# A hybrid decoder step: the first inverse level of the recurrence on VectorE, another order of its value products, longer column fills, query columns behind the last preparation

## The chip, the core and the metric

The kernel runs on one core of one Trainium2 chip. The metric is the device time of one execution in microseconds (us). Before the change the median of three runs is 954.7 us (953.11, 954.70 and 957.25).

## What is computed

One layer of a decoder reads 1,024 prompt positions of width 1,024 and eight single-token samples. After an RMS norm, one projection w_in yields the columns of three head groups: sparse attention (NSA) with 8 query heads, a memory attention, and RWKV-7, a recurrence with 4 heads of 64. Their gated outputs go through w_out. The change touches the recurrence:

```python
def step(s, inp):
    r_t, k_t, v_t, w_t, kk_t, b_t = inp
    sa = jnp.einsum('bhvk,bhk->bhv', s, -kk_t)
    s = s * w_t[:, :, None, :] + sa[..., None] * b_t[:, :, None, :] + v_t[..., None] * k_t[:, :, None, :]
    return s, jnp.einsum('bhvk,bhk->bhv', s, r_t)
s_fin, ys = lax.scan(step, s0, xs)
```

The kernel works in chunks of 64 positions instead of single ones. Inside a chunk the coupling of the positions is a triangular 64 by 64 matrix per head, and the chunk needs its inverse.

## The kernel before

**Phase 1** (about the first 480 us) projects the columns, in tiles of 128 columns, and runs the recurrence between them. The 1,024 positions are four quarters, Q = 0 to 3. For each quarter `rwkv_prep` forms decays, keys and the products AM of one chunk position with another (p_am in PSUM, masked into AM by VectorE at L824), and `rwkv_state` inverts, solves and moves the state on. A quarter has four chunks: two pairs t, and in each pair two chunks p, on the upper or the lower 64 partitions. With four heads h that makes 16 triangular matrices at a time.

**The inverse** has levels. The 64 by 64 matrix is cut into two diagonal blocks of 32 by 32, and within these, levels i = 0 to 4 join blocks of 1, 2, 4, 8 and 16. All 32 blocks of 32 by 32 lie side by side as one tile of 128 partitions by 8 by 32. Level i is: product p_iy = AM times T (32 small matmuls of 32 by 32), mask on VectorE into iY (L857), a fill, product p_it of iY with the transposed T (32 matmuls again), copy by ScalarE into T (L895) and transposition by VectorE into Tt (L896), a fill. Level 0 is shorter: T is the identity there, its product copies AM into PSUM, the mask follows, and the result only has to be transposed (L878). Then come the joining of the two 32-blocks (p_iy and p_it with 16 matmuls each), p_x (inverse times right-hand sides), p_g, and four rounds of p_z (the state) with p_yy (outputs). Between the steps, work that does not wait for the inverse is placed: p_bt (turned keys), and p_r, the products with the values V (L872; 8 matmuls of 64 by 64 for a pair t).

**Order of the work.** TensorE's instructions run in the order in which `InOrder` receives them. `drive` (L598) takes a piece of the recurrence; the piece yields a number n, and `drive` then draws n times SLACK (1.3) us of column projections from the generator `columns` before the next piece. A step of `columns` counts as 0.7. These projections (p_pr, three matmuls for each 128 rows of input) are called fills. ORDER lists the column tiles in the order in which they are drawn: 0 to 5 keys and values, 6 to 9 queries (four tiles), 10 and 11 memory queries, 12 gates, 13 to 20 output gates z. The first EARLY = 17 are drawn beside the recurrence, the other four later.

A projected query tile is worked on for each half H of the positions: ScalarE copies it out, TensorE turns it (p_tk), ScalarE squares it (L375), then VectorE runs `norm_rope`: a reduction (L377), an inverse square root of 12 small instructions (L126 to L137), two multiplications (L383, L384) and six for the rotation (L396 to L399). SyncE stores it (L439). A z tile costs VectorE one or two instructions (L319) per half. Each tile of weights is split into two parts by ScalarE (whi, L283) and VectorE (wlo, L284).

For the other engines a scheduler sets the order; within an engine everything runs in that order, so one instruction that waits holds up all that stand behind it. The scheduler ranks what the recurrence issues ahead of the columns' work. PSUM tiles of the recurrence rotate through three buffers (pool pw).

After Q = 3, `rwkv_close` stores the state (S_out, on SyncE's queue), the pools of the recurrence end, and key blocks are read back (kd, SyncE) for the attention of phase 2; phase 3 is the output projection.

Of the kernel before, what the change touches and what calls it, by code (L numbers as in the profile page):

```python
# [10 lines left out]
F32 = mybir.dt.float32  # L11
# [9 lines left out]
T = 1024  # L21
# [7 lines left out]
ORDER = [4, 1, 11, 2, 3, 6, 5, 7, 13, 17, 10, 9, 15, 8, 0, 14, 12, 18, 16, 19, 20]  # L29
# [19 lines left out]
def bc(ap, shape):  # L49
    return ap.to_broadcast(shape)  # L50
# [64 lines left out]
class Step:  # L115
# [566 lines left out]
    def rwkv_open(self):  # L682
# [8 lines left out]
        self.eye = cm[:, 448:480]  # L691
        self.wa2 = c.tile([128, 256], F32, name="wa2")
# [135 lines left out]
    def rwkv_state(self, Q):  # L828
# [6 lines left out]
        blocks = [(2 * p + b, slice(p * 64 + b * 32, p * 64 + b * 32 + 32), p, b) for p in range(2) for b in range(2)]  # L835
        for g, o, p, b in blocks:
            x = AM[o, 2 * p:2 * p + 2, :, b * 32:b * 32 + 32]
            V.tensor_tensor(x, x, bc(self.eye[o, None, None, :], [32, 2, 4, 32]), op=OP.add)
        th = [(t, h, t * 4 + h) for t in range(2) for h in range(4)]
        bkT, pre = [None] * 2, {}  # L840
        for t in range(2):
            pt = self.pw.tile([128, 4, 64], F32, name="p_at", tag="w")
            for c in range(2):
                PE.transpose(pt[:, 2 * c:2 * c + 2, :].rearrange("p a b -> p (a b)"),
                             ar[:, c, t, 0].rearrange("p s e -> p (s e)"), I[:])
            pre[t] = self.rs.tile([128, 4, 128], F32, name="R", tag=f"R{t}")
            A.activation(pre[t][:, :, 0:64], pt[:], AF.Copy)
        yield 1.0
        T = Tt = None
        for i in range(5):  # L850
# [6 lines left out]
            V.tensor_tensor(Y[:], ps[:], bc(self.levels[:, i:i + 1, :], [128, 8, 32]), op=OP.mult)  # L857
            if i < 2:
                t = i
                pb = self.pw.tile([128, 2, 2, 128], F32, name="p_bt", tag="w")  # L860
                for c in range(2):
                    for p in range(2):
                        PE.transpose(pb[:, c, p, :], bk[:, c, 2 * t + p].rearrange("p a b -> p (a b)"), I[:])
                bkT[t] = self.rs.tile([128, 2, 2, 128], F32, name="bkT", tag=f"bkT{t}")
                A.activation(bkT[t][:], pb[:], AF.Copy)
            elif i < 4:
                t = i - 2
                pr = self.pw.tile([128, 4, 64], F32, name="p_r", tag="w")
                for p in range(2):
                    o, k = slice(p * 64, p * 64 + 64), slice(64 - p * 64, 128 - p * 64)  # L870
                    for h in range(4):
                        PE.matmul(pr[o, h, :], AM[k, 2 * p + t, h, 0:64], UV[k, 2 * t + p, h, :], start=True, stop=True)  # L872
                A.activation(pre[t][:, :, 64:128], pr[:], AF.Copy)
            yield 0.7
            new = [self.ri.tile([128, 8, 32], F32, name="iT", tag=f"iT{j}", bufs=2) for j in range(2)]
            flat = lambda x: x[:].rearrange("p j e -> p (j e)")
# [21 lines left out]
            yield 0.7  # L898
# [10 lines left out]
        yield 0.8  # L909
# [6 lines left out]
        yield 0.8  # L916
# [14 lines left out]
        for t in range(2):  # L931
# [18 lines left out]
            yield 0.7  # L950
# [1447 lines left out]
def host_consts():  # L2398
# [74 lines left out]
```

## Time and profile before

| | us |
|---|---|
| median of three runs | 954.7 |
| the profiled execution, its own time | 954.09 |
| its span, first to last instruction | 952.2 |
| TensorE (PE) busy in it | 914.3 |
| VectorE (DVE) busy | 647.6 |
| ScalarE (ACT) busy | 435.9 |
| the four calls of `rwkv_state`, about | 98 to 142, 183 to 227, 288 to 333, 372 to 419 |

The granted clock of TensorE is 0.996 of full speed over the span. Times in the trace are counted from the span's start. In the timeline a row joins several instructions; its second number is the time from the start of the first to the end of the last, and neighbouring rows of PE overlap at their ends, so the cost of a group is read from its start to the start of the next group. The trace counts two records for each matmul on plain f32 operands: 32 matmuls are x64. In square brackets stands idle time ahead of a row and what ended it.

### The profile page before, as it was taken

How to read it: one execution, taken by the hardware profiler on the slowest of the kernel's cores; microseconds unless marked ns; L12 is line 12 of the kernel's file. 1: busy time of each engine (PE TensorE's matmuls, PEld its weight loads, DVE VectorE, ACT ScalarE, POOL GpSimd, SP SyncE). 2: the span in 40 equal slices, each digit the busy share in tenths (PEclk: the TensorE clock that was granted, in tenths of full speed). 3: DMA queues.
4: the chain of work that ended last, by engine and by line, in shares of the span. 5: the costliest groups of instructions: out<-in, count | busy, mean ns of one | idle time of the engine just before them, and what ended most of it. 6: DMA issues, size and time to landing. Idle time of an engine off the chain costs nothing.

```text
span 952.2 us, 24814 instructions
## 1 busy us (share of the span) xinstructions
PE 914.3 (96%) x9911; PEld 779.8 (82%) x9911; DVE 647.6 (68%) x2017; ACT 435.9 (46%) x979; POOL 178.7 (19%) x270
## 2 busy tenths in 40 slices
PE   8999999999999998999998899999999999999998
PEld 7998888868888787787876788788888887887976
DVE  7668579837593699673447866757677996548564
ACT  7564324232442243222434676576666775424311
POOL 2000000000000000000001453454345665212111
PEclk9999999999999999999999999999999999999999
DMA  8421305221421116137436623251210035976661
GB/s 277 132 68 37 100 13 143 59 54 45 115 79 59 35 56 166 54 84 194 111 90 177 193 69 124 72 170 30 70 41 7 11 112 133 349 240 210 189 238 47
DMA packets 134987, 105.94 MB, mean 111 GB/s; under 512 B 34673, under 2 KB 121272, under 8 KB 134744
## 3 DMA queue, kind: packets, MB, share of 16 engines
q1 hardware_dynamic: 129880, 92.64, 33.2%
q0 software_dynamic: 3200, 10.49, 3.1%
q8 instruction: 78, 1.28, 0.5%
q10 hardware_dynamic: 1792, 1.23, 0.4%
q14 instruction: 37, 0.30, 0.1%
HBM read 85.74 MB, written 22.78 MB: 114 GB/s over the span
## 4 chain that ended last, share of the span: by engine, by line
PE 72%; DVE 16%; ACT 6%; DMA 3%; issue 2%; POOL 1%; SPq 0%; DVEq 0%; ACTq 0%; POOLq 0%
PE p_pr L87 20%; PE p_out L87 9%; PE p_pr L307 7%; PE p_s L87 5%; PE p_pT L87 4%; PE p_o L87 4%; PE p_hid L87 3%; ACT p L1399 2%; DVE p L1398 2%; PE p_z L87 2%; PE p_iy L87 2%; PE p_sc L87 1%; PE p_it L87 1%; PE p_tk L87 1%; PE p_q L87 1%
## 5 line engine op out<-in xcount | busy, mean ns | idle before, releaser
L87 PE MATMUL p_pr<-h,whi 128*128 128x512 f32 (+2 forms) x976 | 238.1, 337 | 0.0
L87 PEld LDWEIGHTS p_pr<-h,whi 128*128 128x128 f32 x976 | 158.1, 189 | 16.2 <-issue 2.2
L87 PE MATMUL p_pr<-h,wlo 128*128 128x512 f32 (+2 forms) x488 | 157.5, 326 | 0.6 <-DVE wlo L284 0.6
L1424 POOL TENSOR_SCALAR p<-p,fac,gates 128x640 f32<-128x640 f32 (+7 forms) x128 | 103.7, 821 | 106.8 <-DVE fac L1421 59.9
L1399 ACT ACTIVATE p<-p,nm 128x640 f32<-128x640 f32 (+7 forms) x128 | 93.0, 728 | 53.6 <-DVE nm L1398 46.1
L87 PEld LDWEIGHTS p_pr<-h,wlo 128*128 128x128 f32 x488 | 91.6, 189 | 9.1 <-DVE wlo L284 0.8
L87 PE MATMUL p_pT<-ident,p 128*128 128x128 f32 x528 | 71.9, 281 | 5.0 <-ACT pt L1369 1.6
L1073 POOL MEMSET w2d<- 128x128 f32 x1 | 0.2, 206 | 397.0 <-DVE rq_t L136 397.0
L1398 DVE CUSTOM_DVE_ANT_0 p<-p_s,bmask 128x512 f32<-128x512 f32 (+7 forms) x96 | 60.3, 661 | 18.5 <-PE p_s L87 16.6
L87 PEld LDWEIGHTS p_pT<-ident,p 128*128 128x128 f32 x528 | 57.7, 142 | 16.0 <-issue 6.4
L307 PE MATMUL p_pr<-h,whi 128*128 128x264 f32 (+2 forms) x320 | 68.3, 309 | 0.4 <-ACT whi L283 0.4
L87 PE MATMUL p_o<-pt,vs 128*64 128x128 f32 x1056 | 67.9, 277 | 0.4 <-DVE cat L1457 0.4
L87 PE MATMUL p_s<-kh,qs 128*128 128x512 f32 (+3 forms) x191 | 65.5, 355 | 1.0 <-DVE nm L1398 1.0
L284 DVE TENSOR_TENSOR wlo<-wraw,whi 128x1024 fp32r<-128x1024 f32 x33 | 40.4, 1223 | 33.3 <-ACT whi L283 33.2
L87 PEld LDWEIGHTS p_o<-pt,vs 128*64 128x64 f32 x1056 | 57.0, 137 | 7.2 <-issue 3.8
L87 PE MATMUL p_s<-kl,qs 128*128 128x512 f32 (+3 forms) x192 | 60.4, 335 | 0.0
L283 ACT ACTIVATE whi<-wraw 128x1024 fp32r<-128x1024 f32 x34 | 36.0, 1058 | 53.4 <-PE p_pr L87 43.8
L1371 DVE COPY pt<-p_pT 128x512 f32<-128x512 f32 (+1 forms) x72 | 48.3, 674 | 13.8 <-PE p_pT L87 13.1
L307 PEld LDWEIGHTS p_pr<-h,whi 128*128 128x128 f32 x320 | 51.1, 189 | 3.2 <-ACT whi L283 0.8
L87 PE MATMUL p_out<-woh,chi 128*128 128x512 f32 x128 | 51.7, 404 | 0.0
L87 PE MATMUL p_out<-woh,clo 128*128 128x512 f32 x128 | 50.2, 392 | 0.4 <-DVE clo L2311 0.4
L87 PE MATMUL p_out<-wol,chi 128*128 128x512 f32 x128 | 49.9, 390 | 0.0
(553 smaller groups left out, 1921.8 us busy)
## 6 DMA issues: line engine op xcount, KB each, us to landing
wraw<-in_w_in_dram SPq DMA_DIRECT2D x34, 512.0 KB
pg<-in_c_pool_dram SPq DMA_DIRECT2D x32, 256.0 KB
pg<-in_c_pool_dram SPq DMA_DIRECT2D x48, 128.0 KB
x<-in_x_prompt_dram SPq DMA_DIRECT2D x8, 512.0 KB
z_d<-zt SPq DMA_DIRECT2D x16, 256.0 KB
cat<-z_d SPq DMA_DIRECT2D x8, 512.0 KB
xres<-in_x_prompt_dram POOLq DMA_DIRECT2D x16, 256.0 KB, 3.7
out_dram<-xres POOLq DMA_DIRECT2D x16, 256.0 KB, 3.0
```

Source lines behind the costliest of these rows:

```text
L87: self.last = getattr(self.engine, op)(*a, **k)
L283: nc.scalar.activation(hi[:, :, :n], raw[:, :, :n], AF.Copy)
L284: (low or nc.vector).tensor_tensor(lo[:, :, :n], raw[:, :, :n], hi[:, :, :n].bitcast(F32), op=OP.subtract)
L307: self.last_mm = self.pe.matmul(ps[:m, :b - a], w[:, k, :m], h[k][:, a:b], start=(k == 0 and i == 0), stop=(k == 7 and i == 2))
L1073: nc.gpsimd.memset(w2d[:], 0.0)
L1371: nc.vector.tensor_copy(pt[:, :n], ps[:, :n])
L1398: V.tensor_tensor_reduce(halves(x), halves(ps), m, -1.0, 3.0e38, op0=OP.add, op1=OP.min, accum_out=nm[:, h, b:b + 1])
L1399: A.activation(x, x, AF.Exp, scale=-1.0, bias=nm[:, h, b:b + 1], accum_out=sm[:, h, b:b + 1])
L1424: nc.gpsimd.tensor_scalar(x, x, f[:, h, b:b + 1], gate[:, hd + h, 1 + b:2 + b], op0=OP.mult, op1=OP.mult)
```

## The change

Four edits:

1. **Level 0 without matmuls.** The mask of level 0 is stored turned over (s < c), under the name `pairs`. VectorE multiplies the 32-blocks of AM by it directly into Tt (four instructions, one for each block of 32 partitions, next to the four that add the identity) and transposes Tt into T. The 32 matmuls of level 0, their mask instruction and the old transposition are gone; the loop runs over i = 1 to 4.
2. **p_bt of the first pair** is issued ahead of the levels, that of the second pair at level 1.
3. **p_r** runs over the heads outside and the two partition halves inside.
4. **Fills and columns.** Most yields between levels grow from 0.7 or 0.8 to 1.0, the first from 1.0 to 1.7, those after p_g from 0.7 to 1.1. For one quarter the yields of `rwkv_state` add up to 16.1 and were 12.5. In ORDER, query tiles 9 and 8 come behind tiles 15 (z) and 0 (keys).

```diff
-ORDER = [4, 1, 11, 2, 3, 6, 5, 7, 13, 17, 10, 9, 15, 8, 0, 14, 12, 18, 16, 19, 20]
+ORDER = [4, 1, 11, 2, 3, 6, 5, 7, 13, 17, 10, 15, 0, 9, 8, 14, 12, 18, 16, 19, 20]
...
+        self.pairs = cm[:, 256:288]
...
+        flat = lambda x: x[:].rearrange("p j e -> p (j e)")
+        T, Tt = (self.ri.tile([128, 8, 32], F32, name="iT", tag=f"iT{j}", bufs=2) for j in range(2))
         for g, o, p, b in blocks:
             x = AM[o, 2 * p:2 * p + 2, :, b * 32:b * 32 + 32]
             V.tensor_tensor(x, x, bc(self.eye[o, None, None, :], [32, 2, 4, 32]), op=OP.add)
+            V.tensor_tensor(Tt[o].rearrange("p (t h) e -> p t h e", t=2), x, bc(self.pairs[o, None, None, :], [32, 2, 4, 32]),
+                            op=OP.mult)
+        V.transpose(flat(T), flat(Tt))
...
-        yield 1.0
-        T = Tt = None
-        for i in range(5):
+        turn_bk(0)
+        yield 1.7
+        for i in range(1, 5):
             ps = self.pw.tile([128, 8, 32], F32, name="p_iy", tag="w")
             for t, h, j in th:
                 for g, o, p, b in blocks:
-                    PE.matmul(ps[o, j, :], AM[o, 2 * p + t, h, b * 32:b * 32 + 32], T[o, j, :] if i else I[o, o],
-                              start=True, stop=True)
+                    PE.matmul(ps[o, j, :], AM[o, 2 * p + t, h, b * 32:b * 32 + 32], T[o, j, :], start=True, stop=True)
             Y = self.ri.tile([128, 8, 32], F32, name="iY", bufs=2)
             V.tensor_tensor(Y[:], ps[:], bc(self.levels[:, i:i + 1, :], [128, 8, 32]), op=OP.mult)
-            if i < 2:
...
+            if i == 1:
+                turn_bk(1)
             elif i < 4:
                 t = i - 2
                 pr = self.pw.tile([128, 4, 64], F32, name="p_r", tag="w")
-                for p in range(2):
-                    o, k = slice(p * 64, p * 64 + 64), slice(64 - p * 64, 128 - p * 64)
-                    for h in range(4):
+                for h in range(4):
+                    for p in range(2):
+                        o, k = slice(p * 64, p * 64 + 64), slice(64 - p * 64, 128 - p * 64)
                         PE.matmul(pr[o, h, :], AM[k, 2 * p + t, h, 0:64], UV[k, 2 * t + p, h, :], start=True, stop=True)
                 A.activation(pre[t][:, :, 64:128], pr[:], AF.Copy)
-            yield 0.7
+            yield 1.0
...
-            if i == 0:
-                V.transpose(flat(new[1]), flat(Y))
-                T, Tt = Y, new[1]
-                continue
...
-            yield 0.7
+            yield 1.1
...
-        rw[:, 256 + i * 32:288 + i * 32] = (s == c) | ((s // (2 * n) == c // (2 * n)) & (s // n != c // n) & (s > c))
+        below = s > c if i else s < c
+        rw[:, 256 + i * 32:288 + i * 32] = (s == c) | ((s // (2 * n) == c // (2 * n)) & (s // n != c // n) & below)
```

How this moves the instructions is shown at three places. First TensorE's queue at the start of `rwkv_state` for Q = 0 (p_at turns the right-hand sides, p_tk a column tile; the numbers in h are buffers):

```order
 L87 MATMUL p_at<-ident,ar 128x128 x4
+L87 MATMUL p_bt<-ident,bk 128x128 x4
 L87 MATMUL p_pr<-h_1_670,whi 128x512
 L87 MATMUL p_pr<-h_1_671,whi 128x512
@@ -566,6 +567,4 @@
 L87 MATMUL p_pr<-h_2_811,whi 128x512
 L87 MATMUL p_pr<-h_2_810,wlo 128x512
-L87 MATMUL p_iy<-ident,AM 32x32 x32
-L87 MATMUL p_bt<-ident,bk 128x128 x4
 L87 MATMUL p_pr<-h_3_813,whi 128x512
 L87 MATMUL p_pr<-h_3_814,whi 128x512
```

The group p_iy<-ident is gone, p_bt stands ahead of the fill, and the twelve rows of fill that were cut in two are one piece ahead of level 1.

Second VectorE's queue in Q = 3, up to the mask of level 1. Before, behind the four additions of the identity (L838), up to the mask L857 of level 1 (mx is the memory group's input, which is normed here):

```order
L133 SCALAR_TENSOR_TENSOR rq_t<-rq_r,rq_a 128x1
L137 SCALAR_TENSOR_TENSOR rq_r<-rq_t,rq_r 128x1
L1120 TENSOR_SCALAR mx_6372<-mx_6372,rq_r 128x1024
L377 TENSOR_REDUCE nr_ss<-nr_sq 128x8
L126 TENSOR_SCALAR rq_a<-nr_ss 128x8
L127 TENSOR_SCALAR rq_g<-rq_a 128x8
L128 TENSOR_SCALAR rq_a<-rq_a 128x8
L135 TENSOR_TENSOR rq_t<-rq_g 128x8
L136 TENSOR_TENSOR rq_t<-rq_t,rq_a 128x8
L137 SCALAR_TENSOR_TENSOR rq_r<-rq_t,rq_g 128x8
L284 TENSOR_TENSOR wlo<-wraw,whi 128x1024
L857 TENSOR_TENSOR iY<-p_iy,c_rw 128x256
```

and now the last rows ahead of that mask, which is L871 in the changed file:

```order
L136 TENSOR_TENSOR rq_t<-rq_t,rq_a 128x8
L137 SCALAR_TENSOR_TENSOR rq_r<-rq_t,rq_r 128x8
L133 SCALAR_TENSOR_TENSOR rq_t<-rq_r,rq_a 128x1
L383 TENSOR_TENSOR nr_y<-p_tk,rq_r 128x512
L137 SCALAR_TENSOR_TENSOR rq_r<-rq_t,rq_g 128x8
L137 SCALAR_TENSOR_TENSOR rq_r<-rq_t,rq_r 128x1
L384 TENSOR_TENSOR nr_y<-nr_y,gains 128x512
L871 TENSOR_TENSOR iY<-p_iy,c_rw 128x256
L396 TENSOR_TENSOR nr_sq<-nr_y,rope 128x8x32
```

Between the transposition L844 and this mask stand 22 instructions now: one L377, one L383, one L384 and 19 small ones. From here to the end of `rwkv_state` four tiles' halves of `norm_rope` are spread over the queue; before there were two.

Third VectorE's queue in Q = 2, where the two 32-blocks are joined. Before:

```order
L890 STREAM_TRANSPOSE iT<-p_it 128x256
L892 COPY Ti<-p_it 32x8x32
L908 COPY iY<-p_iy 32x256
L892 COPY Ti<-p_it 32x8x32
L915 COPY Ti<-p_it 32x8x32
```

and now:

```order
L893 STREAM_TRANSPOSE iT<-p_it 128x256
L137 SCALAR_TENSOR_TENSOR rq_r<-rq_t,rq_r 128x8
L135 TENSOR_TENSOR rq_t<-rq_r 128x8
L136 TENSOR_TENSOR rq_t<-rq_t,rq_a 128x8
L895 COPY Ti<-p_it 32x8x32
L137 SCALAR_TENSOR_TENSOR rq_r<-rq_t,rq_r 128x8
L383 TENSOR_TENSOR nr_y<-p_tk,rq_r 128x512
L284 TENSOR_TENSOR wlo<-wraw,whi 128x1024
L911 COPY iY<-p_iy 32x256
L895 COPY Ti<-p_it 32x8x32
```

The transposition L890 is L893 in the changed file, L892 is L895 and L908 is L911. Nothing of the columns stood between them; now the end of an inverse square root, L383 and a wlo do, since other columns are being projected at this point.

More of the change, by code (lines that the diff above doesn't have):

```diff
@@ L838, in rwkv_state, with turn_bk @@
             V.tensor_tensor(x, x, bc(self.eye[o, None, None, :], [32, 2, 4, 32]), op=OP.add)
+            V.tensor_tensor(Tt[o].rearrange("p (t h) e -> p t h e", t=2), x, bc(self.pairs[o, None, None, :], [32, 2, 4, 32]),
+                            op=OP.mult)
+        V.transpose(flat(T), flat(Tt))
         th = [(t, h, t * 4 + h) for t in range(2) for h in range(4)]
         bkT, pre = [None] * 2, {}
+        def turn_bk(t):
+            pb = self.pw.tile([128, 2, 2, 128], F32, name="p_bt", tag="w")
+            for c in range(2):
+                for p in range(2):
+                    PE.transpose(pb[:, c, p, :], bk[:, c, 2 * t + p].rearrange("p a b -> p (a b)"), I[:])
+            bkT[t] = self.rs.tile([128, 2, 2, 128], F32, name="bkT", tag=f"bkT{t}")
+            A.activation(bkT[t][:], pb[:], AF.Copy)
         for t in range(2):
@@ L868, in rwkv_state @@
                 pr = self.pw.tile([128, 4, 64], F32, name="p_r", tag="w")
-                for p in range(2):
-                    o, k = slice(p * 64, p * 64 + 64), slice(64 - p * 64, 128 - p * 64)
-                    for h in range(4):
+                for h in range(4):
+                    for p in range(2):
+                        o, k = slice(p * 64, p * 64 + 64), slice(64 - p * 64, 128 - p * 64)
                         PE.matmul(pr[o, h, :], AM[k, 2 * p + t, h, 0:64], UV[k, 2 * t + p, h, :], start=True, stop=True)
                 A.activation(pre[t][:, :, 64:128], pr[:], AF.Copy)
-            yield 0.7
+            yield 1.0
             new = [self.ri.tile([128, 8, 32], F32, name="iT", tag=f"iT{j}", bufs=2) for j in range(2)]
-            flat = lambda x: x[:].rearrange("p j e -> p (j e)")
-            if i == 0:
-                V.transpose(flat(new[1]), flat(Y))
-                T, Tt = Y, new[1]
-                continue
             ps = self.pw.tile([128, 8, 32], F32, name="p_it", tag="w")
@@ L897, in rwkv_state @@
                 T, Tt = new
-            yield 0.7
+            yield 1.0
         lo, up = [blocks[0][1], blocks[2][1]], [blocks[1][1], blocks[3][1]]
@@ L908, in rwkv_state @@
         V.tensor_copy(Y[up[1]], ps[up[1]])
-        yield 0.8
+        yield 1.0
         ps = self.pw.tile([128, 8, 32], F32, name="p_it", tag="w")
@@ L915, in rwkv_state @@
         V.tensor_copy(Ti[lo[1], :, 32:64], ps[lo[1]])
-        yield 0.8
+        yield 1.0
         W = [None] * 2
@@ L949, in rwkv_state @@
                                 ar[:, :, t, 1, p, :], op=OP.add)
-            yield 0.7
+            yield 1.1
         ys = []
```

6 lines of the change are left out of this document (removed).

## The prediction

> **What bounds the kernel now.** I read the page first: its busy shares and the chain that ended last.
>
> ```profile
> span 952.2 us, 24814 instructions
> PE 914.3 (96%) x9911; PEld 779.8 (82%) x9911; DVE 647.6 (68%) x2017; ACT 435.9 (46%) x979; POOL 178.7 (19%) x270
> PE 72%; DVE 16%; ACT 6%; DMA 3%; issue 2%; POOL 1%; SPq 0%; DVEq 0%; ACTq 0%; POOLq 0%
> ```
>
> TensorE is busy for 96% of the span, so two things can shorten the kernel: less TensorE work, or less of its 38 us of idle time. The second view is the busy time of each engine in the four calls of `rwkv_state`, Q = 0 to 3.
>
> ```profile
> core 0: us, PE busy (x) PEld busy (x) DVE busy (x) ACT busy (x) POOL busy (x), PEclk, DMA share, GB/s
> 98.00:134.00 36.00, 35.81 (x879) 29.65 (x880) 21.85 (x64) 11.10 (x26) 0.00 (x0) 1.00 0.17 50
> 184.00:220.00 36.00, 32.91 (x827) 24.52 (x826) 18.97 (x47) 11.38 (x24) 0.00 (x0) 1.00 0.23 61
> 288.00:330.00 42.00, 40.44 (x919) 33.98 (x919) 19.94 (x54) 10.66 (x24) 0.00 (x0) 0.96 0.15 41
> 364.00:414.00 50.00, 44.69 (x965) 36.90 (x965) 35.65 (x111) 14.83 (x32) 0.00 (x0) 1.00 0.39 98
> ```
>
> Window minus PE busy is TensorE's idle time: 0.2, 3.1, 1.6 and 5.3 us, together 10.2. Of the 38 us the change can reach only these. The waits of TensorE from 85 to 425 us (engine, line and what it waited for: total, times, longest) say who ends them:
>
> ```profile
> PE p_g L87 <- DVE GT L948: 2.2, 2, 1.3
> PE p_iy L87 <- DVE rq_t L135: 1.8, 1, 1.8
> PE p_r L87 <- issue: 0.9, 1, 0.9
> PE p_iy L87 <- issue: 0.9, 1, 0.9
> PE p_iy L87 <- DVE iY L857: 0.8, 1, 0.8
> PE p_am L87 <- DVE AM L824: 0.8, 1, 0.8
> ```
>
> It is VectorE, and not because the step is long: critical instructions stand in its queue behind the columns' work. So what matters is how much TensorE work goes, and what then stands ahead of the next step on VectorE.
>
> **TensorE work that goes.** From the timeline (a group's cost is its start to the next group's start):
>
> ```profile
> 102.06 0.75 PE L87 MATMUL p_iy<-ident,AM 32*32 32x32 f32 x64
> 102.75 0.66 PE L87 MATMUL p_bt<-ident,bk 128*128 128x128 f32 x4
> 103.16 0.72 PE L87 MATMUL p_pr<-h,whi 128*128 128x512 f32 x2
> 104.73 0.75 PE L87 MATMUL p_iy<-iY,AM 32*32 32x32 f32 x64
> 114.15 0.96 PE L87 MATMUL p_r<-UV,AM 64*64 64x64 f32 x16
> 115.05 0.51 PE L87 MATMUL p_pr<-h,whi 128*128 128x256 f32 x2
> 125.91 2.09 PE L87 MATMUL p_x<-R,Ti 64*64 64x128 f32 x32
> 127.93 0.73 PE L87 MATMUL p_pr<-h,whi 128*128 128x512 f32 x2
> 129.47 0.46 PE L87 MATMUL p_g<-AM,W 64*64 64x64 f32 x16
> 129.87 0.50 PE L87 MATMUL p_pr<-h,whi 128*128 128x512 f32 x1
> 410.53 0.60 PE L87 MATMUL p_z<-UV,bkT 128*128 128x128 f32 x4
> 410.97 0.61 PE L87 MATMUL p_z<-Zn,PT 128*128 128x128 f32 x4
> ```
>
> *Level 0* costs 102.75 - 102.06 = 0.69 us in each quarter: **-2.8** in four. A change of shape costs a little more: the six rows of fill from 103.16 to 104.73 take 1.57 with one such change, and I take 0.1 for it, four times: **-0.4**. This is certain work off the bounding engine.
>
> *p_r* takes 0.90 us (114.15 to 115.05) with its four products of one partition half in a row. The nearest rows have the halves in turn, as p_r will. p_g<-AM has the same shape and count and takes 0.40, but its halves go to two PSUM tiles. p_x goes to one tile, as p_r does: 2.02 us for 32 records with 128 columns, so a quarter of it, 0.51, for 16 records with 64. p_r should come to 0.40 to 0.51 and save 0.39 to 0.50; I take 0.45, between the two, eight times: **-3.6** (-3.1 to -4.0).
>
> The Trainium skill (TensorEngine Tiling (Array Packing), Restrictions and Gotchas) speaks against this: matmuls on different row tiles cannot work into one PSUM bank at the same time. By it p_r stays at 0.90 and the 3.6 us are lost. The trace disagrees: a p_z group needs 0.44 us for 4 full-height records of 128 columns, 0.11 each, so 32 of p_x one by one would be 3.5 us, not 2.02.
>
> The fills are only moved: the same projections run earlier. p_bt is moved too, at its 0.41. Total TensorE work: -6.8.
>
> **What VectorE gets.** Durations by shape, from 98 to 420 us (group: busy, mean ns), and two small instructions in a row:
>
> ```profile
> L284 DVE TENSOR_TENSOR wlo<-wraw,whi 128x1024 fp32r<-128x1024 f32 x20 | 24.4, 1222 | 16.7 <-ACT whi L283 16.6
> L383 DVE TENSOR_TENSOR nr_y<-p_tk,rq_r 128x512 f32<-128x512 f32 x14 | 9.6, 688 | 0.3
> L377 DVE TENSOR_REDUCE nr_ss<-nr_sq 128x8 f32<-128x512 f32 x14 | 9.5, 682 | 5.6 <-ACT nr_sq L375 5.6
> L396 DVE TENSOR_TENSOR nr_sq<-nr_y,rope 128x256 f32<-128x256 f32 x20 | 8.4, 420 | 0.1
> L838 DVE TENSOR_TENSOR AM<-AM,c_rw 32x256 f32<-32x256 f32 x16 | 6.7, 417 | 0.4
> L896 DVE STREAM_TRANSPOSE iT<-p_it 128x256 f32<-128x256 f32 x12 | 5.4, 446 | 13.8 <-ACT iT L895 13.8
> ```
>
> ```profile
> 376.75 0.17 DVE L126 TENSOR_SCALAR rq_a<-nr_ss 128x8 f32<-128x8 f32 x1
> 376.96 0.17 DVE L127 TENSOR_SCALAR rq_g<-rq_a 128x8 int32<-128x8 int32 x1
> 378.86 0.42 DVE L857 TENSOR_TENSOR iY<-p_iy,c_rw 128x256 f32<-128x256 f32 x1
> ```
>
> The four products by `pairs` have the shape of L838, 0.42 each; a mask (0.42) and one transposition (0.45) go, one transposition comes. So +1.3 us of VectorE in each quarter, and between the last mask of AM and level 1 stand eight block instructions (3.5) and a transposition (0.45), 4.0 us. Dependent small ones follow each other by 0.2, so one half of a `norm_rope` costs 0.7 + 12 x 0.2 + 2 x 0.7 + six rotations at about 0.34 (they overlap) = 6.5 us.
>
> *Q = 0.* Two masks (1.3) and the 4.0 make 5.3 us behind p_am. TensorE has 15 rows of fill (2.2), p_at and p_bt (0.8) and 12 rows (2.9) ahead of level 1: 5.9. Hidden, with 0.6 to spare; without that cover it would cost up to the 4.0. Idle stays near 0.2.
>
> *Q = 1.* I add up both queues from p_rs on. VectorE: preparation and an L377 3.4, small ones 2.4, L383, L384 and L377 2.1, rotation 2.0, masks 1.2, small ones 2.3, masks 1.2, L383 0.7, block instructions 3.5, L384 0.7, transposition 0.45: 20.0. TensorE: fills, p_tk and p_am to p_bt, then 12 rows, 17.9 with 0.35 of waiting for a buffer. Idle 2.1 + 0.35, about 2.5. Before it is 3.1, of which about 0.8 is records missing in the trace: **+0.2**.
>
> *Q = 2.* In the joining of the blocks (third place of the order) the second copy of Ti now stands behind L383 and wlo: from the end of p_iy of level 4, VectorE reaches L893 at 3.3, the first copy at 4.4, is through with L383 and wlo at 6.8 and with the two copies at 7.7, where p_it can start. TensorE is there after p_tk 0.4, fill 1.4, p_it 0.7, fill 1.4, p_iy 0.6 and fill 0.7: at 5.3. A new wait of 2.4. The 1.3 us ahead of p_g go (L948 no longer stands behind L383). **+1.1**.
>
> *Q = 3* is where the query columns now fall. VectorE before: 35.65 us busy in 50. Two more halves of `norm_rope` (13) and the 1.3 make 50.0, while TensorE has 44.69 - 0.7 - 0.9 + 1.3 x 3.6 (longer yields) = 47.8. So **VectorE becomes the bound of this stage**, and at the least 2.2 us of idle follow. At the most VectorE's waiting of before (50 - 35.65 = 14.4) stays beside all its work: 50.0 + 14.4 - 47.8 = 16.6. Between the two I follow the queue. The L1123 norm of the memory input now stands ahead of the masks; its DMA must land and be squared:
>
> ```profile
> 364.55 1.06 ACT L1118 ACTIVATE sqm<-mx 128x1024 bf16<-128x1024 f32 x1 [3.45 <-DMA mx<-in_mem_prompt_dram]
> ```
>
> That holds VectorE until 10 us behind p_rs; p_am, p_bt and level 1 wait about 1.2 together. Then L377, L383, L384 and 19 small ones (0.12 each where two chains alternate) make 4.2 ahead of level 1's mask, where TensorE offers p_iy, p_bt and a fill, 2.5: wait 2.0. In the same way 1.35 ahead of p_it of level 2, 0.3 of level 3, 1.2 of level 4 (a wlo in it), 0.5 and 0.4 in the joining and p_g. Sum 6.9 against 5.3 before: **+1.6** (from -3.1 to +11.3). The preparation of Q = 3 shows no idle that the move could win back.
>
> *Behind Q = 3* about 4.4 us of fill are left where 13 were. SyncE's queue must pass the last output stores (about 8 us behind the last Zn) and S_out before it reads the first keys:
>
> ```profile
> 434.56 0.44 PE L1014 MATMUL p_s<-ident,Zn 128*128 128x128 f32 x2
> 442.56 0.60 PE L1241 MATMUL p_k<-ident,kd 128*128 128x128 f32 x4
> ```
>
> Eight us of TensorE work lie between these two, now as before, and the keys come some 14 us behind Zn: **+0.3** (0 to 1.5). The four query stores (L439) also stand later on SyncE, ahead of a weight load of the last columns; those have a buffer and some 12 us of work in hand, so nothing.
>
> **Sum.** -2.8 - 0.4 - 3.6 + 0.2 + 1.1 + 1.6 + 0.3 = -3.6 us, against the profiled execution's 954.09: 950.5. The median is 0.6 above it: **951.0**.
>
> **Rivals.**
> *The covers hold.* The waits of Q = 2 and Q = 3 depend on the moment at which two queues meet, and longer fills give every step 0.4 us more or better. If Q = 3 has only the 2.2 that its loads force, and Q = 2 nothing new: -6.8 + 0.2 - 1.3 - 3.1 + 0.3 = -10.7; halfway -7, so 944 to 949.5. For it: waits of this kind are few before (one of 1.8, one of 1.3). Against: the same rows show that one wlo in the way is enough.
> *Slower: Q = 3 is bound by VectorE with its pauses.* The inverse asks for VectorE twice at each level and TensorE for its answer, so VectorE's 14.4 us of waiting need not fill up with the new norms. At +11.3 there, the sum is +6.1: 961. It turns to slower than before where Q = 3 idles more than 3.6 us above the 6.9, that is over 10.5. For it: VectorE at 50.0 in a stage of 48. Against: the added norms are what the pauses can hold.
> *p_r gains nothing*, since both halves write one PSUM tile: -3.6 + 3.6 = 0, 954.6. p_x speaks against it.
>
> **Chances.** The forecast (half of the VectorE waits come back) 0.50, 948 to 953.5; covers hold 0.32; p_r without gain 0.08; slower 0.10, six tenths of it past 0.5%. A measurement of this kernel can tell about 0.5%, 4.8 us, from no change: below 949.9 is faster, above 959.5 slower. All of the second case and a fifth of the first: faster 0.42; slower 0.06; same 0.52. Range 945 to 956.5: it leaves out the lower end of the covers and most of the slower case.
>
> **What would show it.** Right: no p_iy<-ident group, p_r near 0.45 instead of 0.90, TensorE busy about 907.5; in Q = 3 VectorE busy near 50 us and waits of TensorE on iY or iT behind L383, L384 or wlo; in Q = 2 a wait of p_it on Ti or iY. Wrong: p_r at 0.9; VectorE with over 10 us of pauses in Q = 3; a wait of p_k on kd over 2 us; a wait in the preparations.

## The result, and the profile after

The changed kernel takes **949.6 us** (median of 13 executions, 947.7 to 952.8); the kernel before, executed beside it, 956.9 (13 executions). The ratio is 0.9932, with a 95% interval of 0.9917 to 0.9947: 6.5 us, or 0.7%, faster. The forecast was 951.0, with a range of 945 to 956.5 that holds the result. The profiled execution took 948.73 us with a span of 946.9. The page's first lines, of the changed kernel:

```profile
span 946.9 us, 24305 instructions
PE 911.0 (96%) x9655; PEld 776.5 (82%) x9655; DVE 656.6 (69%) x2029; ACT 436.5 (46%) x979; POOL 179.5 (19%) x270
```

TensorE is busy for 3.3 us less, in a span that is 5.3 us shorter. The busy times in the four calls of `rwkv_state`, in the same stretches as before (columns: stretch, its length, PE, PEld, DVE, ACT, POOL, the granted clock, DMA share and GB/s):

```profile
98.00:134.00 36.00, 35.92 (x809) 29.82 (x809) 25.18 (x77) 12.65 (x28) 0.00 (x0) 1.00 0.17 49
184.00:220.00 36.00, 34.10 (x769) 25.43 (x769) 20.49 (x48) 12.74 (x26) 0.00 (x0) 0.95 0.23 61
288.00:330.00 42.00, 38.77 (x844) 33.33 (x843) 21.69 (x65) 10.90 (x24) 0.00 (x0) 0.96 0.15 40
364.00:414.00 50.00, 47.42 (x919) 39.18 (x918) 43.85 (x150) 15.82 (x33) 0.00 (x0) 1.00 0.44 100
```

TensorE's idle time is now 0.1, 1.9, 3.2 and 2.6 us, together 7.8 instead of 10.2. Q = 3 gained 2.7, Q = 2 lost 1.7. The largest waits of TensorE from 85 to 425 us, changed kernel (total, times, longest):

```profile
PE p_it L87 <- DVE iY L871: 2.2, 3, 1.3
PE p_it L87 <- DVE Ti L895: 1.9, 2, 1.7
PE p_iy L87 <- DVE iT L844: 1.7, 1, 1.7
PE p_r L87 <- issue: 1.6, 1, 1.6
```

The waits of p_g, p_am, p_at and p_x that stood in the kernel before are gone or small. In their place stand p_iy on the new transposition (L844), p_it on Ti (L895) and on the masks (L871), and one stop of 1.6 us within p_r that waits for no other engine. Such a stop, which the profile puts down to "issue", is called a pause in what follows.

**One stretch for all kernels.** From the first p_rs to the first p_k of the first keys lies all that the change touches. It took 357.1 us before (85.4 to 442.5: busy 346.9, idle 10.2) and takes 349.9 now (85.3 to 435.2: busy 341.8, idle 8.1). So 7.2 us go there: 5.0 of work and 2.1 of idle time. Of these, 5.3 are left at the end of the span. About 0.5 goes to p_k's wait for the keys, 0.56 before and 1.03 now:

```profile
PE p_k L1244 <- DMA kd<-k_d: 1.0, 1, 1.0
```

Set against the same matmuls of the kernel before, the changed kernel's lead is 6.7 us behind that wait, 6.2 from 540 us on and 6.0 at its last matmul (942.3 against 948.4); the last 0.7 goes behind it. In these parts the two kernels are the same.

**Times at one clock.** The granted clock differs from execution to execution, in 203 timed executions from 0.982 up to 0.998, and within each kernel the time falls by 0.61 us for each 0.001 of it (one slope fitted to all of them). That is as large as the effects in question, so beside the ratios I give each kernel's mean time brought to a clock of 0.995 by this slope, with its standard error. It is a reading of mine, not a measurement by itself, and it has a limit: the clock is not independent of the kernel. In the traces it falls to half for 3.4 us at a time, mostly just behind a long wait of TensorE (last section), so a kernel that waits more also tends to get less clock, and this column takes that part of a wait's cost out. Where the two columns disagree, the ratio is the measurement. For the rest the column is steady: the kernel before comes out at 956.4 to 956.9 on the four occasions on which it was executed beside the others, 956.7 over all. "Work" and "idle" are TensorE's in the stretch above, and "pauses" the part of the idle time that waits for no other engine.

| kernel | ratio to before (95%) | us at clock 0.995 | work | idle | pauses |
|---|---|---|---|---|---|
| before | 1 | 956.7 | 346.9 | 10.2 | 2.5 |
| changed | 0.9932 (0.9917 to 0.9947) | 948.8 ± 0.3 | 341.8 | 8.1 | 1.6 |
| order_back | 0.9928 (0.9902 to 0.9955) | 950.0 ± 0.3 | 339.8 | 10.8 | 2.9 |
| fills_back | 0.9965 (0.9942 to 0.9988) | 952.4 ± 0.4 | 341.4 | 12.1 | 4.7 |
| halves_back | 0.9930 (0.9911 to 0.9949) | 950.3 ± 0.3 | 345.7 | 7.3 | 1.4 |
| level0_back | 0.9936 (0.9915 to 0.9958) | 949.9 ± 0.3 | 343.8 | 5.2 | 0 |
| level0_alone | 1.0033 (1.0014 to 1.0052) | 958.2 ± 0.4 | 346.4 | 14.3 | 5.9 |
| fills_alone | 0.9974 (0.9960 to 0.9987) | 952.3 ± 0.5 | 345.3 | 5.2 | 0.6 |
| level0_alone_spread | 1.0061 (1.0039 to 1.0083) | 958.2 ± 0.7 | 349.6 | 14.2 | 5.2 |
| together_vector | 0.9931 (0.9912 to 0.9950) | 945.9 ± 0.6 | 344.3 | 8.0 | 0 |
| together_tensor | 0.9945 (0.9920 to 0.9970) | 950.3 ± 0.4 | 350.3 | 7.8 | 1.6 |
| fills_longer | 0.9971 (0.9946 to 0.9997) | 950.3 ± 0.5 | 356.9 | 8.5 | 2.1 |

In the last three rows more columns are worked off ahead of p_k, so their work is not to be compared with the others'. Work, idle time and pauses come from one execution of each kernel. The work carries that execution's clock: the changed kernel's has two stretches of 3.4 us at half clock in it, the one before has one, and by an estimate from these lengths its work at the same clock would be another 1.7 us less. How far idle time and pauses scatter shows *halves_two_tiles* below: it has the changed kernel's order of work on TensorE, and 9.7 us of idle time with 3.2 of pauses where the changed kernel has 8.1 with 1.6. A difference of that size in one row says little by itself.

### The profile page after: what moved, and what is told of

It reads as the page before. It is cut to its first block, busy times and chain, and to the rows that moved or that the text cites. A ratio compares the mean times of both kernels' runs of the same rounds, so it can differ in the third digit from the quotient of the medians.

```text
span 946.9 us, 24305 instructions
## 1 busy us (share of the span) xinstructions
PE 911.0 (96%) x9655; PEld 776.5 (82%) x9655; DVE 656.6 (69%) x2029; ACT 436.5 (46%) x979; POOL 179.5 (19%) x270
## 3 DMA queue, kind: packets, MB, share of 16 engines
q8 instruction: 76, 1.25, 0.5%
## 4 chain that ended last, share of the span: by engine, by line
PE 71%; DVE 16%; ACT 6%; DMA 3%; issue 2%; POOL 1%; SPq 0%; DVEq 0%; ACTq 0%; POOLq 0%
PE p_pr L87 20%; PE p_out L87 9%; PE p_pr L307 7%; PE p_s L87 5%; PE p_pT L87 4%; PE p_o L87 4%; PE p_hid L87 3%; ACT p L1402 3%; DVE p L1401 2%; PE p_z L87 2%; PE p_sc L87 1%; PE p_it L87 1%; PE p_tk L87 1%; DVE pt L1374 1%; PE p_q L87 1%
```

## The experiments

**The four parts, each undone alone.** These kernels were executed side by side with the one before, not beside the changed one, so they are compared with it through the ratio or the one-clock column.

*order_back.* The columns stand as before:

```diff
-ORDER = [4, 1, 11, 2, 3, 6, 5, 7, 13, 17, 10, 15, 0, 9, 8, 14, 12, 18, 16, 19, 20]
+ORDER = [4, 1, 11, 2, 3, 6, 5, 7, 13, 17, 10, 9, 15, 8, 0, 14, 12, 18, 16, 19, 20]
```

> The changed kernel with the column order of before; all else as changed. Theory A (the forecast's step for Q = 3: the query columns' norms load VectorE there and cost TensorE idle): with them back ahead of the last preparation, TensorE's idle time of Q = 3, 2.6 us in the changed kernel's trace, falls to about 1, and about 1 comes back in Q = 2: the time is 0 to 2 us lower than the changed kernel's, about 948.5. Rival B (the place of the columns is itself a gain, since in the kernel before Q = 3 idled 5.3 us at other work): idle of Q = 3 goes back to about 5, the time is 2 to 4 us higher, 952 to 954.

The ratio cannot be told from the changed kernel's; at one clock it is 1.2 us slower, with 2.7 us more idle time, of which 1.3 are pauses. Theory A falls: with the query columns back, Q = 3 idles more, not less (3.6 us from 364 to 414, VectorE busy 33.0). Two rows of VectorE and one of TensorE, order_back, show why:

```profile
371.13 0.15 DVE L126 TENSOR_SCALAR rq_a<-ss_m 128x1 f32<-128x1 f32 x1 [2.84 <-ACT sqm L1121]
...
374.51 1.28 DVE L825 TENSOR_TENSOR AM<-p_am,c_rw 128x512 f32<-128x512 f32 x2
```

```profile
375.25 0.44 PE L87 MATMUL p_at<-ident,ar 128*128 128x128 f32 x2 [2.65 <-DVE AM L825]
```

VectorE stands for 2.84 us on the square of the memory input, and the second masks of AM are queued behind it, its small instructions and a wlo; p_at waits 2.65 for them. In the changed kernel the same wait falls ahead of p_am and hides:

```profile
365.11 0.15 DVE L126 TENSOR_SCALAR rq_a<-ss_m 128x1 f32<-128x1 f32 x1 [4.61 <-ACT sqm L1121]
...
367.68 1.28 DVE L825 TENSOR_TENSOR AM<-p_am,c_rw 128x512 f32<-128x512 f32 x2
```

Rival B has the sign, by the one-clock column alone, and not the size (1.2 for 2 to 4). So the place of the query columns is worth about a microsecond. The two traces put it down to where the memory input's wait falls; the norms do cost TensorE something in the changed kernel (2.2 us of p_it waiting for iY), but less than that wait of 2.65.

*fills_back.* The fill lengths as before:

```diff
-        yield 1.7
+        yield 1.0
...
-            yield 1.0
+            yield 0.7
...
-            yield 1.1
+            yield 0.7
```

> The changed kernel with the fill lengths of before between the steps of the inverse and the joining (0.7 and 0.8 in place of 1.0, 0.7 in place of 1.1, the first 1.0 in place of 1.7). Theory A (the longer fills cover VectorE's answers): the sum of TensorE's waits between the first p_rs and the first p_k, 8.1 us in the changed kernel's trace, rises by 4 to 8, most of it as p_it waiting for iY and p_iy for iT; 953 to 957. Rival B (the waits are set by what stands ahead in VectorE's queue; the same columns only run later): within 1.5 us of the changed kernel.

At one clock 3.6 us slower (by the ratio 3.2), the largest of the four, and 4.0 us more idle time: theory A. But its form was not the one expected. TensorE's waits, fills_back, 85 to 436 us:

```profile
PE p_iy L87 <- issue: 3.3, 3, 1.9
PE p_iy L87 <- DVE iT L844: 2.7, 3, 1.6
PE p_it L87 <- DVE iY L871: 2.2, 3, 1.6
PE p_g L87 <- DVE GT L951: 1.7, 3, 0.6
PE p_it L87 <- issue: 1.5, 1, 1.5
```

Of the 4.0 us, 3.1 are pauses; the last section shows what they are.

*halves_back.* p_r with a half's four products in a row (`for p` outside `for h`).

> The changed kernel with the four products of one partition half of p_r in a row, as before. Theory A (what the changed trace shows, 0.61 us for a p_r in place of 0.90): p_r takes 0.90 again and the time is 2.3 us higher, 951 to 953. Rival B (the forecast's 0.45): 3.6 us higher, with the same 0.90. Rival C (the order saves nothing on the path, since the fills behind p_r only start sooner and the next answer of VectorE is waited for instead): p_r 0.90, TensorE's waits 1.5 to 2.3 us less, the time within 1 us.

p_r takes 0.89 us again (109.86 to 110.75). The group of all eight, changed kernel, and the same of halves_back:

```profile
L87 PE MATMUL p_r<-UV,AM 64*64 64x64 f32 x128 | 5.7, 224 | 1.6 <-issue 1.6
```

```profile
L87 PE MATMUL p_r<-UV,AM 64*64 64x64 f32 x128 | 8.0, 224 | 1.4 <-issue 1.4
```

That is 2.3 us of TensorE; 0.8 comes back as less idle time, and at one clock it is 1.5 us slower. The ratio cannot be told from the changed kernel's. Theory A is right about p_r; that the time gains less than 2.3 fits theory C in part, by which a shorter p_r also shortens the cover of VectorE's answer, but 0.8 of idle time is within the scatter.

*level0_back.* Level 0 as 32 products by the identity on TensorE, with mask and transposition, and its fill of 0.7 taken from the first 1.7:

```diff
-            V.tensor_tensor(Tt[o].rearrange("p (t h) e -> p t h e", t=2), x, bc(self.pairs[o, None, None, :], [32, 2, 4, 32]),
-                            op=OP.mult)
-        V.transpose(flat(T), flat(Tt))
...
-        yield 1.7
-        for i in range(1, 5):
+        yield 1.0
+        for i in range(5):
...
+            if i == 0:
+                V.transpose(flat(new[1]), flat(Y))
+                T, Tt = Y, new[1]
+                continue
```

> The changed kernel with the first level of the inverse on TensorE again (32 products by the identity, mask, transposition), the same total length of fills around it, p_bt still ahead of the levels. Theory A (the level's removal is worth its TensorE time): TensorE works 3.3 us more between the first p_rs and the first p_k (p_iy 18.1 in place of 14.8), VectorE 5.2 us less, of which at most the 1.7 us wait of p_iy for iT in Q = 1 comes back: the time is 1.5 to 3.5 us higher, 951 to 953. Rival B (VectorE's queue sets the pace of these stages, so its 1.3 us in each quarter come back as less waiting): within 1 us of the changed kernel or below.

The ratio cannot be told from the changed kernel's; at one clock it is 1.1 us slower. In the stretch to p_k the products of level 0 are there again (the p_iy groups 18.1 us against 14.8), and the idle time is 2.9 us less, as the wait of 1.65 us for the new transposition and the pause of 1.6 are gone. (The stretch as a whole is even 0.9 us shorter, but the changed kernel's profile has one half-clock stretch more in it.) So rival B is right for most of it: of the 3.3 us of products that the change takes off TensorE, a third or less is left.

**Two parts alone, on the kernel before.**

*level0_alone.* Only level 0 on VectorE (and p_bt's places); order, fills and p_r as before, the sum of the fills unchanged (1.7 ahead of level 1, then 0.7).

> The kernel before with only the first level moved to VectorE (with p_bt of the first half ahead of the levels, p_bt of the second at level 1); column order, fill lengths and p_r as before, the total length of fills unchanged. Theory A (VectorE's queue sets the pace of these stages, as the run with level 0 back on TensorE says): TensorE works 3.3 us less between the first p_rs and the first p_k, its waits grow by 2.5 to 4, mostly as p_iy of level 1 waiting for iT; the time is within 1 us of before or up to 2 us above. Rival B (the forecast's steps, -2.8 - 0.4 + 0.2 + 1.1): 2 to 3.5 us faster than before.

Slower than before: 1.3 to 5.0 us by the ratio's interval, 1.5 at one clock. The forecast's steps (rival B) are out. Theory A has the sign, and the idle time grows by 4.1, about as it said, but its cause is not what the trace shows: 3.4 of them are pauses, and p_iy of level 1 waits 0.3 us for iT. The largest waits of level0_alone:

```profile
PE p_r L87 <- issue: 4.7, 2, 2.4
PE p_g L87 <- DVE GT L951: 2.2, 2, 1.3
PE p_it L87 <- DVE iY L871: 1.5, 1, 1.5
```

*fills_alone.* Only the longer fills (1.0 in place of 0.7 and 0.8, 1.1 behind p_g; level 0's as they were).

> The kernel before with only the longer fills (level 0's two fills as they were, 1.0 and 0.7; 1.0 at the other steps, 1.1 behind p_g). Theory A (the longer fills are the largest single part of the gain, as the run with short fills in the changed kernel says): TensorE's work the same, its waits between the first p_rs and the first p_k, 10.2 us before, fall by 3 to 4.5, the time by 2.5 to 4 us. Rival B (longer fills pay only where level 0 is off TensorE, or with the query columns moved): within 1 us of before.

Faster, by 1.2 to 3.8 us by the interval and 4.4 at one clock, with 5.0 us less idle time: theory A. Its waits, 85 to 442 us:

```profile
PE p_it L87 <- DVE Ti L892: 1.9, 2, 1.7
PE p_at L87 <- DVE AM L824: 1.1, 1, 1.1
```

The wait of p_it on Ti is there without the other parts: it comes with the longer fills, not with level 0.

**What holds p_r at 0.61 us.** Two versions of the changed kernel. *halves_two_tiles*: a PSUM tile for each half. *halves_four_quarters*: two tiles, and heads in turn to the one and the other half of the columns.

```diff
-                        PE.matmul(pr[o, h, :], AM[k, 2 * p + t, h, 0:64], UV[k, 2 * t + p, h, :], start=True, stop=True)
+                        PE.matmul(prs[p][o if h % 2 == 0 else k, h, :], AM[k, 2 * p + t, h, 0:64], UV[k, 2 * t + p, h, :], start=True, stop=True)
```

> The changed kernel with a PSUM tile for each partition half of p_r (and a copy for each half). Theory A (one PSUM tile for both halves is what holds p_r at 0.61): p_r takes 0.40 to 0.45, like p_g's products. Rival B (two pairs of row and column halves in turn are two streams whatever the tiles; p_g's products use four): 0.61 as before.

> The changed kernel with p_r as p_g's products stand: a PSUM tile for each half of the rows, and heads in turn to the one and the other half of the columns, so that four pairs of row and column halves take turns (two more copies on ScalarE for each p_r). Theory A (one PSUM tile holds p_r): 0.40 to 0.45, the same as with two tiles alone. Rival B (the number of pairs sets it): 0.40 here, where two tiles alone leave 0.61. Rival C (what p_r reads sets it): 0.61 in both.

One p_r and the group behind it: changed kernel, two tiles, four quarters.

```profile
114.41 0.68 PE L87 MATMUL p_r<-UV,AM 64*64 64x64 f32 x16
115.02 0.65 PE L87 MATMUL p_tk<-ident,ct 128*128 128x128 f32 x4
```

```profile
114.99 0.68 PE L87 MATMUL p_r<-UV,AM 64*64 64x64 f32 x16
115.60 0.66 PE L87 MATMUL p_tk<-ident,ct 128*128 128x128 f32 x4
```

```profile
114.61 0.46 PE L87 MATMUL p_r<-UV,AM 64*64 64x64 f32 x16
115.00 0.66 PE L87 MATMUL p_tk<-ident,ct 128*128 128x128 f32 x4
```

0.61, 0.61 and 0.39: rival B. (Their one execution each, 951.6 and 953.0 us, tells nothing of the time.) A second tile changes nothing; the number of row and column quarters that take turns sets it. The Trainium skill (TensorEngine Tiling (Array Packing), Tiling Modes) has four independent tiles of 64 x 64, and these rows agree: one quarter at a time 0.89, two 0.61, four 0.39. The rule of the Trainium skill on row tiles and one PSUM bank (TensorEngine Tiling (Array Packing), Restrictions and Gotchas) is not what limits p_r here: one PSUM tile or two, it takes 0.61.

**Is it the pauses that make level 0 alone slower?** *level0_alone_spread*: p_r leaves levels 2 and 3 for the two joining steps and as much fill goes the other way.

```diff
-            yield 0.7
+            yield 1.5 if i in (2, 3) else 0.7
...
+        p_r(0)
-        yield 0.8
+        yield 0.2
```

> The kernel before with the first level on VectorE alone, as in the run of that kind, but the two p_r of each quarter trade places with as much fill: they leave levels 2 and 3 (fill there 1.5 in place of 0.7) and stand in the two joining steps (fill there 0.2 in place of 0.8). The same work on every engine. Theory A (TensorE's pauses that wait for no other engine, 5.9 us in the run with level 0 alone against 2.5 before, end 2.3 to 2.7 us after the start of a packet of the instruction queue; they come where short products stand close together, and are what made level 0 alone slower): with fewer instructions in a row these pauses fall to 3 or less and the time by 2 to 4 us, to between 3 us below before and before. Rival B (VectorE's queue made it slower): the pauses on VectorE stay at 8, the time stays 2 to 4 us above before.

It does not tell the two apart. The pauses did not fall (5.2 against 5.9); they moved, from p_r to p_iy (2.0 and 0.7 us) and even into fills (1.3 twice). The other waits stayed as well (9.0 against 8.4). At one clock the time is that of level0_alone, and by the ratio it is 3.7 to 7.9 us above before. Placing p_r elsewhere is no remedy. What makes level 0 alone slower is told apart in its trace only (3.4 us more of pauses, 0.7 of other waits), and not by an experiment that took the pauses away.

**Versions that might be faster still.** *together_vector*: the changed kernel with Ti's four copies of level 4 on ScalarE, p_r in four quarters, and p_r in the joining steps with 1.4 of fill at levels 2 and 3 and 0.7 at the joining. *together_tensor*: the same with level 0 on TensorE.

```diff
-                    (V.tensor_copy if g % 2 else A.copy)(self.Ti[o, :, b * 32:b * 32 + 32], ps[o])
+                    A.copy(self.Ti[o, :, b * 32:b * 32 + 32], ps[o])
```

> The changed kernel with three things more: the four copies into Ti of level 4 all on ScalarE (two were VectorE's), p_r as products of four quarters in two PSUM tiles, and p_r in the joining steps with as much fill in its place at levels 2 and 3. Theory A (VectorE's queue and p_r's length still cost): p_r 0.40, 1.7 us of TensorE work less, the wait of p_it on Ti of 1.65 us in Q = 2 gone, TensorE's idle time between the first p_rs and the first p_k 5 in place of 8.1: 3 to 5 us below the changed kernel, a ratio to before of 0.988 to 0.990. Rival B (the waits only move to the next answer of VectorE or ScalarE, whose copies now stand ahead of p_x): within 1 us of the changed kernel.

> The same three things with level 0 on TensorE (as in the run with level 0 back). Theory A (what level 0 on VectorE saves TensorE, 3.3 us, comes back as waiting): the same time as its twin with level 0 on VectorE within 1.5 us, TensorE's idle time between the first p_rs and the first p_k 2 to 4 us less and its work 3.3 us more. Rival B (with the copies of Ti off VectorE and p_r spread, VectorE has room for level 0): its twin is 2 to 3.3 us faster.

By the ratio, together_vector is the changed kernel's equal (949.8 us); rival B by that measure. The wait of p_it on Ti is gone, and others stand in its place:

```profile
PE p_pr L87 <- DVE zt L319: 2.0, 1, 2.0
PE p_iy L87 <- DVE rq_t L135: 1.9, 1, 1.9
PE p_r L87 <- ACT Ti L898: 1.0, 1, 1.0
PE p_g L87 <- DVE UV L936: 0.9, 1, 0.9
```

At one clock it would be 2.8 us faster, but all its six executions had a clock of 0.987 to 0.991 (mean 0.989, the changed kernel's 0.9935). Whether the kernel itself brings that clock about stays open, so no gain is claimed. The twin with level 0 on TensorE is 1.3 us slower by the ratio, which its interval does not tell from none and which is within theory A's 1.5, and 4.4 at one clock, which rests on the same low clock of together_vector. Its idle time is not less (7.8 against 8.0), against theory A. Whether level 0 on VectorE begins to pay with room made there stays open; the sign is rival B's.

*fills_longer*: the changed kernel with 1.4 in place of 1.0 at every step.

> The changed kernel with longer fills again: 1.4 in place of 1.0 at every step of the inverse from level 1 on and in the joining. Theory A (the fills are what gives VectorE's answers and TensorE's instruction packets their time, as the step from 0.7 to 1.0 did): TensorE's idle time between the first p_rs and the first p_k falls from 8.1 to 4 to 5.5 us, the pauses that wait for no other engine to 0 to 1 of it; 2 to 4 us below the changed kernel, a ratio to before of 0.989 to 0.991. Rival B (what is left does not come from fills that are too short: wlo and norms ahead in VectorE's queue, loads that land late): the idle time stays at 7 to 9 or moves behind Q = 3, where the columns now run out; within 1.5 us of the changed kernel or above.

Rival B: a ratio of 0.9971, above the changed kernel's 0.9932, with intervals that just touch. Idle time stays at 8.5, and behind Q = 3 the columns are used up, so that p_k waits for its keys (fills_longer, from 437 us):

```profile
PE p_k L1244 <- DMA kd<-k_d: 3.7, 4, 1.8
```

The first p_k stands at 451.2 us; the mean clock was 0.988. Of the three lengths tried, 0.7, 1.0 and 1.4, 1.0 is the best here. Why 1.4 is worse is not told apart: the columns that run out and the lower clock both stand in its trace.

## Why the forecast held, step by step

The number held (951.0 against 949.6) and the sign with it, but that it came this close is in part luck: the terms are off by more than the sum, and their errors partly cancel. Q = 3 came out 4.3 us better than forecast and Q = 1 1.4 better; p_r saved 1.3 less and Q = 2 cost 0.6 more. And the longer fills, worth 3.6 to 4.4 us, stood in the sum at nothing; what they bring shows in the stages' waits, so it is not to be added to the errors above. The gain was just past what a measurement can tell (0.53 to 0.83%), where I had given 0.42 to faster and 0.52 to no difference. By its number the result lies in the forecast's case (948 to 953.5), 0.1 above the end of its neighbour, *the covers hold*. By its mechanism it is a mixture: Q = 3 went nearly as the neighbour has it (2.6 us of idle time where it has 2.2), Q = 2 as the forecast has it.

- *Level 0: -2.8 and -0.4.* The work was right: the groups of p_iy fall from 18.1 us to 14.8. The kernel before, then the changed one:

```profile
L87 PE MATMUL p_iy<-iT,AM 32*32 32x32 f32 x896 | 12.0, 194 | 1.3 <-issue 0.9 <-DVE rq_r L137 0.2 <-ACT iT L895 0.2
L87 PE MATMUL p_iy<-ident,AM 32*32 32x32 f32 x256 | 3.1, 194 | 0.0
L87 PE MATMUL p_iy<-iY,AM 32*32 32x32 f32 x256 | 3.0, 194 | 2.6 <-DVE rq_t L135 1.8 <-DVE iY L857 0.8
```

```profile
L87 PE MATMUL p_iy<-iT,AM 32*32 32x32 f32 x1152 | 14.8, 194 | 1.9 <-DVE iT L844 1.7 <-DVE rq_r L137 0.3
```

  The step that failed is the sentence behind it, "certain work off the bounding engine". TensorE was busy for 96%, but in these stages it also waits, and most of what level 0 gave came back as waiting: at one clock it costs 1.5 us alone, and brings 1.1 as the last part. TensorE's busy time in the whole span is 911.0 instead of the 907.5 that the forecast named; 1.3 of the difference is p_r, about 1.7 (an estimate) the extra half-clock stretch.
- *p_r: -3.6.* Right in kind, mis-sized: -2.3 (0.61 each, outside the 0.40 to 0.51). The two rows that I took for bounds were the wrong neighbours: p_g's products work in four quarters, p_r's in two; and p_x, two quarters like p_r, has 128 columns, of which 64 cost more than half.
- *"The fills are only moved".* This is the term that was missing. Longer fills entered only as TensorE work within Q = 3's sum and, in a rival, as 0.4 us a step. They are worth 3.6 us (taken away) to 4.4 us (alone) at one clock, about half of the gain; by the ratios 3.2 and 2.5.
- *Q = 0 and Q = 1.* 0.2 forecast, 0.1 measured; 2.5 forecast, 1.9 measured, 1.65 of it where I had put it, p_iy of level 1 on the new transposition. One reading was wrong: of the 3.1 us of Q = 1 before, nothing is records missing in the trace (every trace with level 0 on TensorE has the same 9911 matmul records). They are waits for VectorE and ScalarE, 1.7 us, and two pauses of 0.9 and 0.4, so the step is -1.2 and not +0.2.
- *Q = 2: a new wait of 2.4 and 1.3 less ahead of p_g.* Both came. The rows of VectorE and TensorE, changed kernel:

```profile
312.55 0.69 DVE L383 TENSOR_TENSOR nr_y<-p_tk,rq_r 128x512 f32<-128x512 f32 x1
313.16 1.22 DVE L284 TENSOR_TENSOR wlo<-wraw,whi 128x1024 fp32r<-128x1024 f32 x1
314.40 0.43 DVE L911 COPY iY<-p_iy 32x256 f32<-32x256 f32 x1
314.76 0.42 DVE L895 COPY Ti<-p_it 32x256 f32<-32x256 f32 x1
```

```profile
315.23 0.69 PE L87 MATMUL p_it<-Ti,iY 32*32 32x32 f32 x30 [1.65 <-DVE Ti L895]
```

  The copies stand behind L383 and wlo as read from the order; 1.65 us instead of 2.4. fills_alone has the same 1.65 us wait with the old column order, so it is the longer fills that bring these instructions there. The 1.6 us pause in p_r of this stage was not foreseen, and makes the stage's loss 1.7 where 1.1 was forecast.
- *Q = 3: 6.9 us of idle time.* 2.6 measured, the largest error in size. The step that failed is "two more halves of norm_rope (13)" in the stretch from 364 to 414: VectorE is busy 43.85 there, not 50.0. The changed kernel has four L383 and four L377 in it, the kernel before had three and two, so about one and a half halves came and not two whole ones, and chains that run beside each other take less than 0.2 a step. The kernel before, then the changed one, from 364 to 414 us:

```profile
L383 DVE TENSOR_TENSOR nr_y<-p_tk,rq_r 128x512 f32<-128x512 f32 x3 | 2.1, 691 | 0.1
L377 DVE TENSOR_REDUCE nr_ss<-nr_sq 128x8 f32<-128x512 f32 x2 | 1.4, 684 | 2.3 <-ACT nr_sq L375 2.3
```

```profile
L383 DVE TENSOR_TENSOR nr_y<-p_tk,rq_r 128x512 f32<-128x512 f32 x4 | 2.8, 691 | 0.3 <-DVE rq_t L133 0.2
L377 DVE TENSOR_REDUCE nr_ss<-nr_sq 128x8 f32<-128x512 f32 x4 | 2.7, 677 | 0.7 <-ACT nr_sq L375 0.7
```

  The 1.2 us for p_am, p_bt and level 1 behind the memory input came to 0.3. The wait ahead of level 1's p_it stands where it was put, 1.3 instead of 2.0.
- *Behind Q = 3: +0.3.* p_k's wait grew by 0.5.
- *The rivals.* "p_r gains nothing" is out (0.90 to 0.61, and one PSUM tile or two make no difference). The slower case did not come in this kernel. That it was no empty one shows in level0_alone, but there the trace has TensorE's own pauses and not VectorE's.

At one clock the four parts, each undone alone, make 1.2 + 3.6 + 1.5 + 1.1 = 7.4 us, with an error of about 1.3; the whole is 7.9. Within that error the parts add up when taken away from the whole, though level 0, put alone into the kernel before, has the other sign.

## What to carry to other kernels

Work taken off an engine that is busy for 96% pays only where the stage does not wait for something else: look at the stage's own idle time, and try a longer cover before a shorter step. Fill between dependent steps is a term of the sum, not a thing that is only moved; its length is worth a few trials. A price for small matrix products is to be taken from a row with the same number of row and column quarters in turn, not from one of the same shape.

## What the hardware showed that was not expected

**Pauses are late instruction packets.** TensorE's pauses that wait for no engine ("issue") follow its instruction queue. The DMA view lists a queue of the kind "instruction" with 76 packets and 1.25 MB for the changed kernel:

```profile
q8 instruction: 76, 1.25, 0.5%
```

PE and PEld have 19310 records and TensorE's sequencer has 249 more, about 257 for each packet of 16 KB. A pause of level0_alone in Q = 3, and the DMA view of the microsecond from 384.9, and of 386 to 388:

```profile
384.97 0.68 PE L87 MATMUL p_r<-UV,AM 64*64 64x64 f32 x8
387.89 0.68 PE L87 MATMUL p_r<-UV,AM 64*64 64x64 f32 x8 [2.24 <-issue]
```

```profile
q8 instruction: 1, 0.02, 7.2%
```

```profile
DMA packets 0, 0.00 MB, mean 0 GB/s; under 512 B 0, under 2 KB 0, under 8 KB 0
```

TensorE stops in the middle of p_r's sixteen records, with no transfer in flight for most of the pause, and goes on 2.5 us after the start of an instruction packet. In the traces of all 14 kernels there are 29 such pauses within the stretch, from 0.2 to 2.4 us long. Two counts show what they are.

- *Where they fall.* Number the records of PE, PEld and the sequencer in order of time, and count them off in blocks of 256. All 29 pauses end at the record with number 193 or 194 of its block; the 128 waits of over 0.15 us for other engines and for DMA in the same stretches are spread over all numbers. So a pause falls at the border between two blocks of 256 instructions, wherever that lies among the products.
- *What ends them.* Every pause ends 2.2 to 2.8 us after the start of a packet, and it is always the packet that belongs to that border: the n-th packet to the n-th border. The 500 other packets of these stretches were in time: the first record of their block runs 2.3 us or more after the packet's start.

So TensorE has used up its instructions and stands until the next packet is there. What goes wrong is that the packet starts late: in the middle (median) 242 records ahead of its block where no pause came, 109 where one did, and 0 and 2 ahead of the two longest pauses of level0_alone. That packets would be held apart by the queue does not explain it. They start 3.3 us apart or more, but 27 of the 29 that ended a pause started over 3.7 us behind the one before, those of the two longest pauses of level0_alone 11.9 and 13.7 us behind. Why a packet starts late stays open.

This fits what the fills do: a level of the inverse has 256 records in its two groups of products, which alone take 1.4 us (two groups of 0.69), and fills are few records for their time. Pauses were 2.5 us before, 0.6 with longer fills alone, 5.9 with level 0 alone and 4.7 with the changed kernel's fills shortened. That longer fills work by this is not shown separately: they also cover VectorE's answers.

**A wait can cost clock behind it.** In the traces the granted clock of TensorE is either full or half. The changed kernel's wait of 1.65 us for the new transposition ends at 188.5 us, and a stretch at half clock begins 1.3 us later (columns as in the table of stretches above):

```profile
186.40:189.80 3.40, 1.75 (x72) 1.30 (x71) 3.31 (x10) 0.00 (x0) 0.00 (x0) 1.00 0.24 77
189.80:193.20 3.40, 3.40 (x71) 2.37 (x69) 2.04 (x4) 0.60 (x1) 0.00 (x0) 0.50 0.33 90
```

A row of fill with 256 columns takes 0.35 us at full clock (428.60 to 428.95) and 0.64 in the other half-clock stretch, behind the wait for Ti that ends at 315.2 (317.10 to 317.74). In the 14 traces, from the first p_rs to the first p_k, there are 26 such stretches, 23 of them 3.4 us long and three longer. Of these, 22 begin between 0.3 us ahead of and 1.7 us behind the end of a wait of 1.29 us or more; 41 waits were that long, so about half of them brought one. The 116 shorter waits account for the other four. By an estimate from 3.4 us at half clock, each costs up to 1.7 us, as much as the wait itself. So a long wait can cost more than its own length, and a clock that differs between two kernels need not be chance. No run here changes the waits alone, so this rests on the order of time and on these counts.
